# A mixture of experts whose three emptiest experts run with 64 slots

## The chip, the cores and the metric

The kernel runs on one core of one Trainium2 chip. The metric is the device time of one execution in microseconds (us), 1692.99 us as the median of three runs.

The engines are named as the profile names them: PE is TensorE's matrix multiply and PEld its weight load, DVE is VectorE, ACT is ScalarE, POOL is GpSimd and SP is SyncE. SP computes nothing here: its queue issues the loads of the weights.

## The reference

A trunk of two layers on 256 tokens of width 1024, all in float32. The first layer has a gated mixer with forgetting attention, memory cross-attention and a dense SwiGLU; the second has differential attention with a short convolution, memory cross-attention and a mixture of experts. The change lies in the last:

```python
def moe_swiglu(h, w_router, wg, wu, wd):            # h: 256 x 1024
    logits = t @ w_router                            # 8 experts
    top_v, top_i = lax.top_k(logits, 2)
    gates = softmax(top_v)
    combine = sum(one_hot(top_i, 8) * gates[..., None], axis=1)
    for e in range(8):                               # wg[e], wu[e]: 1024 x 3584, wd[e]: 3584 x 1024
        out += combine[:, e:e+1] * ((silu(t @ wg[e]) * (t @ wu[e])) @ wd[e])
```

Each token goes to two experts, so the eight experts share 512 places; on the inputs of the reference they get 42, 47, 42, 111, 102, 72, 34 and 62 tokens.

## The kernel before, in words

All matrix products take float32 data as pairs: a high part rounded to the fast matmul type (fp32r) and a low part, what is left. A product of two split operands is then three matmuls, high by high, high by low and low by high (`mm3`, lines 130 to 142). Activations are split once. Weights come from DRAM as float32 pieces of 1 MB into a buffer called raw, and `load_w` (lines 107 to 123) splits each piece: ACT writes the high part wh in two halves (line 118), DVE the low part wl in one instruction (line 120).

The experts run in the order 0 to 7, and each in seven chunks of 512 of its 3584 inner columns. For each expert the tokens are gathered into 128 slots by a matmul with a one-hot matrix (`slots`, `gather_pair`, `gained`, two experts at once), so that the tokens are the stationary operand, 128 slots wide, split into xgh and xgl, and the weights stream past as 512 columns. A chunk consists of:

- gate and up (`gate_up`): two weight pieces each, 8 matmul steps of 128x512 each, times three;
- `gated`: ACT takes silu of the gate sum and DVE multiplies the up sum into it, into sg, 128 slots x 512;
- `to_hT`: four PE transposes of sg into one PSUM bank (htp), from which ACT writes the high part of hs and DVE the low part (lines 126 and 127);
- `down`: two pieces of the down weights, 8 steps times three, into two PSUM banks that add up over the seven chunks.

In a chunk c the loop (line 1031 on) issues gate and up of c, then the loads and the down step of chunk c-1, then `to_hT` of c. The six pieces of a chunk are called g0, g1, u0, u1, d0 and d1 in the text. hs has a single buffer, so hs of a chunk is written when the down step before has read the last one. The order in which an engine issues its instructions is laid down when the program is built, from the data they need and the buffers that come free; it can differ from chunk to chunk, and each engine then keeps to it.

Buffers set the pace between the engines. Raw pieces go round a ring of 11 places (lines 996 and 997); SP issues a load when the piece that had the place has been split. Split pieces go round four pairs of wh and wl (line 999: three of the pool wsplit and one of wsplit2).

The first expert's slots are worked out in `route` from the router's logits: rank of each expert for each token, mask, and place of the token in its expert (pos). The gates (`gates`) follow in the second chunk. At the very end the largest count is taken (lines 1079 to 1084), every engine loads it as a number (line 1115), and a block that computes what does not fit into 128 slots is skipped when it is at most 128.

Of the kernel before, what the change touches and what calls it, by code (L numbers as in the profile page):

```python
# [20 lines left out]
P = 128  # L21
# [30 lines left out]
@with_exitstack  # L52
def trunk_kernel(ctx: ExitStack, tc: tile.TileContext, io, out, stop=None, cap=CAP):
    nc = tc.nc
# [150 lines left out]
    def route_consts():  # L205
        wr = cp.tile([P, KT, NE], F32, tag="wr", name="wr")
        nc.gpsimd.dma_start(wr, io["router_w"][0].rearrange("(k p) n -> p k n", p=P))
        gc = cp.tile([P, KT], F32, tag="gc", name="gc")
        gcr = t4([KT, P], "gcr")
        nc.gpsimd.dma_start(gcr, io["norm_ffn"][1].rearrange("(k p) -> k p", p=P))  # L210
        gcp = trp.tile([P, KT], F32, tag="tr", name="gcp")
        nc.tensor.transpose(gcp, gcr, ident[0:KT, 0:KT])
        nc.vector.tensor_copy(gc, gcp)
        nc.vector.tensor_tensor(wr, wr, gc[:, :, None].to_broadcast([P, KT, NE]), op=OP.mult)
        tri = cp.tile([P, NE, NE], F32, tag="tri", name="tri")
        nc.gpsimd.memset(tri, 1.0)
# [10 lines left out]
        return wr, gc, tri, ustr, ones, iota  # L227

    pA = ctx.enter_context(tc.tile_pool(name="acts", bufs=1))
    ps2 = ctx.enter_context(tc.tile_pool(name="xs", bufs=2))  # L230
    with ExitStack() as pre:
# [526 lines left out]
        with behind("resid", "Pool"):  # L758
            wr, gc, tri, ustr, ones, iota = route_consts()
        mem_v_half(1, 0)  # L760
# [3 lines left out]
    with ExitStack() as moe:  # L764
# [13 lines left out]
        lgs = mA.tile([P, 2, NE], F32, tag="lgs", name="lgs")  # L778
        rank = mA.tile([P, 2, NE], F32, tag="rank", name="rank")

        rht = pA.tile([P, 2, KT, P], F32, tag="V", name="rht")
# [6 lines left out]
        def route(t, acc):  # L788
# [53 lines left out]
            if t:  # L842
                with behind("pp"):
                    gather(0, 1)
                for i in range(2):
                    gather(1, i)

        def gates():
            for t in range(2):
# [16 lines left out]
                nc.vector.tensor_scalar(comb[:, t, 0:NE], s0, ge[:, 0:1], None, op0=OP.mult)  # L866
                nc.vector.scalar_tensor_tensor(comb[:, t, 0:NE], s1, ge[:, 1:2], comb[:, t, 0:NE], op0=OP.mult, op1=OP.add)

        def slots(dst, t, e):

            chain["DVE"] = nc.vector.tensor_scalar(dst, iota, pos[:, t, e:e + 1], None, op0=OP.is_equal)
            if cap < P:
                nc.vector.memset(dst.bitcast(F32)[..., cap:P], 0.0)

        def gained(kk, dst, src):

            dh, dl = (xg_all[i][:, dst, kk, :] for i in range(2))
            chain["ACT"] = nc.scalar.activation(dh, src, AF.Copy, scale=gc[:, kk:kk + 1])
            chain["DVE"] = nc.vector.scalar_tensor_tensor(dl, src, gc[:, kk:kk + 1], dh.bitcast(F32), op0=OP.mult, op1=OP.subtract)

# [3 lines left out]
        def gather_pair(e):  # L884
# [6 lines left out]
            for q in range(4):  # L891
# [4 lines left out]
                for k in range(2):  # L896
                    kk = 2 * q + k
                    sl = slice(kk * P, (kk + 1) * P)
                    for t in range(2):
                        nc.tensor.matmul(ps[:, k, :, :], xh[t][:, sl], se[:, t, :, :], start=t == 0, stop=False)  # L900
                        nc.tensor.matmul(ps[:, k, :, :], xl[:, t, sl], se[:, t, :, :], start=False, stop=t == 1)
                    gained(kk, slice(0, n), ps[:, k, 0:n, :])

# [27 lines left out]
        def gate_piece(w, e, c, half):  # L931
            return load_w(w[e, half * 512:(half + 1) * 512, c * 512:(c + 1) * 512]
                          .rearrange("(k p) n -> p k n", p=P), 4, 512)

        def gate_up(e, c, xg, ready=(), between=None):
# [3 lines left out]
            for w in (wg, wu):  # L939
# [4 lines left out]
                for half in range(2):  # L944
                    wh, wl = ready.pop(0) if ready else gate_piece(w, e, c, half)
                    mm = mm3([(ps, xgh[:, half * 4 + k, :], xgl[:, half * 4 + k, :], wh[:, k, :], wl[:, k, :])
                         for k in range(4)], False, half == 0, half == 1)
                res.append(ps)
                chain["PE"] = mm
            return res  # L950

        def gated(res, rs):
            sg = m2.tile([P, 512], F32, tag="sg", name="sg", bufs=1)
# [4 lines left out]
        def down_w(e, c, parts=1):  # L958
            return [load_w(wd[e, c * 512 + half * 256:c * 512 + half * 256 + 256, :]
                           .rearrange("(k p) n -> p k n", p=P), 2, D, parts) for half in range(2)]  # L960

        def to_hT(sg, pool=pA, tag="gain"):
            tp = mbank([P, 4, P], "htp")
# [7 lines left out]
        def down(c, hT, yacc, w2, ns=(0, 1)):  # L971
            hh, hl = hT
            return mm3([(yacc[n], hh[:, half * 2 + k, :], hl[:, half * 2 + k, :],
                  w2[half][0][:, k, n * 512:(n + 1) * 512], w2[half][1][:, k, n * 512:(n + 1) * 512])
# [42 lines left out]
        def final_gain():  # L1017
# [10 lines left out]
            return gf  # L1028

        prev = y = st = nrs = pyacc = gf = None  # L1030
        for e in range(NE):
            for c in range(nch):
# [28 lines left out]
                if prev is not None:  # L1061
                    w2 = down_w(*prev[:2])
                sg = gated(gu, rs)
                if prev is not None:
# [7 lines left out]
                if c == 0:  # L1072
                    yacc = [mmp.tile([P, 512], F32, tag="mm", name=f"y{n}") for n in range(2)]
                hT = to_hT(sg) if e + 1 < NE or c + 1 < nch else to_hT(sg, mA, "y")
                prev = (e, c, hT, yacc)
            xg, rs = xg_of(e % 2), nrs

        cc = mbank([P, NE], "cc")
        for t in range(2):
            nc.tensor.matmul(cc, ones, msk[:, t, :], start=t == 0, stop=t == 1)  # L1080
        cmax = sm.tile([P, 1], F32, tag="cmax", name="cmax")
        nc.vector.tensor_reduce(cmax, cc, axis=AX.X, op=OP.max)
        cint = mA.tile([1, 1], I32, tag="cint", name="cint")
        nc.vector.tensor_copy(cint, cmax[0:1, :])
        def finish(gf, before):
# [24 lines left out]
        def last_scatter(n):  # L1110
            scatter(pe, st, split_y(yacc, n, pA, ("gain", "K")[n]), n)
        finish(gf, last_scatter)


        cv = nc.values_load(cint[0:1, 0:1], min_val=0, max_val=S,
                            skip_runtime_bounds_check_because="a count of 256 tokens lies in 0..256")
        with tc.If(cv > cap):
            for e in range(NE):
                for r0 in range(cap, S, P):
                    se = mA.tile([P, 2, P], F32, tag="y", name="se_o")  # L1120
# [3 lines left out]
                    po = sm.tile([P, 2], F32, tag="po", name="po")  # L1124
                    nc.vector.tensor_scalar(po, pos[:, :, e], float(-r0), None, op0=OP.add)
                    for t in range(2):
# [24 lines left out]
                    for c in range(nch):  # L1151
                        sgs = []
                        for w in (wg, wu):
                            ps = accp.tile([P, 4, P], F32, tag="acc", name="gu_o")
                            raws = [load_raw(w[e, half * 512:(half + 1) * 512, c * 512:(c + 1) * 512]
                                             .rearrange("(k p) n -> p k n", p=P), 4, 512) for half in range(2)]
# [8 lines left out]
                        for half in range(2):  # L1165
                            rr = c * 512 + half * 256
                            rw = load_raw(wd[e, rr:rr + 256, :].rearrange("(k p) n -> p k n", p=P), 2, D)
                            for k in range(2):
# [43 lines left out]
```

## Time and profile before

| | us |
|---|---|
| runs, median of 3 | 1692.99 (1690.9 to 1695.35) |
| the profiled execution | 1696.55 |
| its span | 1694.7 |
| from the first gating of expert 0 to the last of expert 7 | about 661 to 1668 |

A profile is one execution of the program on the chip. Busy time of an engine is the time in which it ran instructions, idle time is put down to what released the next instruction. Matmuls overlap, so that PE can be counted busy while it does not run at its peak; the weight loads (PEld) show the pitch. The clock column is the share of TensorE's full clock that was granted. A load counts from its issue to its landing.

### The profile page before, as it was taken

How to read it: one execution, taken by the hardware profiler on the slowest of the kernel's cores; microseconds unless marked ns; L12 is line 12 of the kernel's file. 1: busy time of each engine (PE TensorE's matmuls, PEld its weight loads, DVE VectorE, ACT ScalarE, POOL GpSimd, SP SyncE). 2: the span in 40 equal slices, each digit the busy share in tenths (PEclk: the TensorE clock that was granted, in tenths of full speed). 3: DMA queues.
4: the chain of work that ended last, by engine and by line, in shares of the span. 5: the costliest groups of instructions: out<-in, count | busy, mean ns of one | idle time of the engine just before them, and what ended most of it. 6: DMA issues, size and time to landing. Idle time of an engine off the chain costs nothing. (4 is left out here: it accounts for less than half of the span.)

```text
span 1694.7 us, 22153 instructions
## 1 busy us (share of the span) xinstructions
PE 1649.0 (97%) x8700; PEld 1381.4 (82%) x8700; DVE 1273.6 (75%) x1170; ACT 1059.1 (62%) x1354; POOL 46.0 (3%) x64
## 2 busy tenths in 40 slices
PE   8999999999999999999999999999999999999996
PEld 7799889999988888888888777777778777778774
DVE  6686665444586657989888889788789878888876
ACT  6455554343564448877777676766667767677655
POOL 1000000000000102000000000000000000000000
PEclk9899999999999999999999999999999999999998
DMA  7446456565545577998998999999998999999970
GB/s 237 143 161 223 155 200 210 174 199 174 189 127 190 196 294 272 379 381 324 361 367 311 341 335 329 345 333 343 343 347 321 336 343 335 345 334 333 331 274 27
DMA packets 224556, 464.48 MB, mean 274 GB/s; under 512 B 9074, under 2 KB 64390, under 8 KB 224316
## 3 DMA queue, kind: packets, MB, share of 16 engines
q1 hardware_dynamic: 223564, 459.80, 76.2%
q0 software_dynamic: 880, 3.19, 0.5%
q8 instruction: 70, 1.15, 0.3%
q14 instruction: 42, 0.34, 0.1%
HBM read 461.90 MB, written 2.11 MB: 274 GB/s over the span
## 5 line engine op out<-in xcount | busy, mean ns | idle before, releaser
L120 DVE TENSOR_TENSOR wl<-raw,wh 128x2048 fp32r<-128x2048 f32 (+1 forms) x527 | 983.9, 1895 | 248.8 <-ACT wh L118 244.7
L118 ACT ACTIVATE wh<-raw 128x1024 fp32r<-128x1024 f32 x866 | 848.3, 1047 | 268.4 <-PE pws L138 92.0
L135 PE MATMUL gu<-wh,ch 128*128 128x512 f32 x896 | 357.0, 399 | 1.6 <-ACT wh L118 1.6
L138 PE MATMUL gu<-wh,cl 128*128 128x512 f32 x896 | 353.5, 395 | 0.0
L141 PE MATMUL gu<-wl,ch 128*128 128x512 f32 x896 | 250.3, 401 | 18.0 <-DVE wl L120 17.5
L141 PEld LDWEIGHTS gu<-wl,ch 128*128 128x128 f32 x896 | 162.2, 188 | 80.5 <-DVE wl L120 50.1
L135 PEld LDWEIGHTS gu<-wh,ch 128*128 128x128 f32 x896 | 169.0, 189 | 37.0 <-ACT wh L118 2.5
L138 PEld LDWEIGHTS gu<-wh,cl 128*128 128x128 f32 x896 | 169.0, 189 | 35.8
L135 PE MATMUL y<-wh,hs 128*128 128x512 f32 x448 | 179.3, 400 | 0.9 <-ACT wh L118 0.9
L138 PE MATMUL y<-wh,hs 128*128 128x512 f32 x448 | 177.0, 396 | 0.0
L135 PE MATMUL pws<-nh,wh 128*128 128x256 f32 x560 | 137.1, 283 | 0.0
L138 PE MATMUL pws<-nl,wh 128*128 128x256 f32 x560 | 137.1, 283 | 0.0
L126 ACT ACTIVATE hs<-htp 128x512 fp32r<-128x512 f32 x56 | 33.5, 598 | 142.1 <-PE y L141 116.9
L141 PE MATMUL y<-wl,hs 128*128 128x512 f32 x448 | 118.6, 395 | 0.0
L135 PEld LDWEIGHTS pws<-nh,wh 128*128 128x128 f32 x560 | 105.9, 189 | 1.3 <-ACT wh L118 0.9
L138 PEld LDWEIGHTS pws<-nl,wh 128*128 128x128 f32 x560 | 106.0, 189 | 0.4
L135 PEld LDWEIGHTS y<-wh,hs 128*128 128x128 f32 x448 | 84.3, 188 | 21.9 <-ACT wh L118 1.5
L141 PEld LDWEIGHTS y<-wl,hs 128*128 128x128 f32 x448 | 84.2, 188 | 19.4 <-issue 0.8
L138 PEld LDWEIGHTS y<-wh,hs 128*128 128x128 f32 x448 | 84.4, 188 | 18.5
L135 PE MATMUL acc<-wh,ch 128*128 128x512 f32 x216 | 84.8, 392 | 0.0
L138 PE MATMUL acc<-wh,cl 128*128 128x512 f32 x216 | 84.5, 391 | 0.0
L141 PE MATMUL pws<-nh,wl 128*128 128x256 f32 x560 | 78.9, 283 | 0.0
(329 smaller groups left out, 1786.5 us busy)
## 6 DMA issues: line engine op xcount, KB each, us to landing
raw<-in_moe_w_gate_dram SPq DMA_DIRECT2D x112, 1024.0 KB, 5.7
raw<-in_moe_w_up_dram SPq DMA_DIRECT2D x112, 1024.0 KB, 6.0
raw<-in_moe_w_down_dram SPq DMA_DIRECT2D x110, 1024.0 KB, 6.2
raw<-in_mem_w_kv_dram SPq DMA_DIRECT2D x16, 1024.0 KB, 5.4
raw<-in_odd_w_in_dram SPq DMA_DIRECT2D x12, 1024.0 KB, 5.2
raw<-in_ffn_w_gate_dram SPq DMA_DIRECT2D x11, 1024.0 KB, 5.2
raw<-in_ffn_w_up_dram SPq DMA_DIRECT2D x11, 1024.0 KB, 5.2
raw<-in_ffn_w_down_dram SPq DMA_DIRECT2D x11, 1024.0 KB, 4.8
```

What stands on the lines that cost most here:

```text
L118: chain["wh"] = nc.scalar.activation(hf[:, sl], rf[:, sl], AF.Copy)
L120: chain["wl"] = nc.vector.tensor_sub(lf[:, sl], rf[:, sl], hf[:, sl].bitcast(F32))
L126: return (nc.scalar.activation(hi, src, AF.Copy), nc.vector.tensor_sub(lo, src, hi.bitcast(F32)))
L135: mm = nc.tensor.matmul(ps, ah, bh, start=f, stop=False, skip_group_check=bank)
L138: nc.tensor.matmul(ps, *((ah, bl) if w_left else (al, bh)), start=False, stop=False, skip_group_check=bank)
L141: mm = nc.tensor.matmul(ps, *((al, bh) if w_left else (ah, bl)), start=False, stop=e, skip_group_check=bank)
```

## The change

The experts are put in order on the chip. `places` counts the tokens of each expert, ranks the experts by count (expert 0 always comes first) and spreads them over eight places: the three with the fewest tokens besides expert 0 come to places 2, 4 and 6. Positions, numbers, counts and gates are brought into that order, and SP loads the seven numbers into registers, from which it addresses the weights of places 1 to 7.

An expert at place 2, 4 or 6 has 64 slots. The one-hot matrix holds the 64 slots twice side by side; the high parts of the tokens go to columns 0 to 63 of the stationary tile and the low parts to columns 64 to 127. One matmul with wh and one with wl then give the sum for the high parts in rows 0 to 63 and for the low parts in rows 64 to 127, so two matmuls stand for three (`mm2`; the product of both low parts comes with them). `gated` copies both sums out, and `to_hT` multiplies them with a matrix of two stacked unit matrices (`twice`), which turns and adds the halves; gating and split follow on 64 columns a piece.

The fourth pair of split buffers goes, and the raw ring gets a twelfth place. The block for what does not fit starts at 64 slots for the small places.

```diff
-RAW2 = 3
+RAW2 = 4
+SCAP = 64
+SMALL = (2, 4, 6)
...
-        wp2 = moe.enter_context(tc.tile_pool(name="wsplit2", bufs=1))
...
-        pools["w"] = [wp] * 3 + [wp2]
...
+        def places():
+            cc = mbank([P, NE], "cc")
+            for t in range(2):
+                nc.tensor.matmul(cc, ones, msk[:, t, :], start=t == 0, stop=t == 1)
+            key = sm.tile([P, NE], F32, tag="s0", name="key")
+            nc.vector.scalar_tensor_tensor(key, cc, float(NE), iota[:, 0:NE], op0=OP.mult, op1=OP.add)
+            nc.vector.memset(key[:, 0:1], -1.0)
...
+            nc.vector.tensor_tensor(c1, key[:, None, :].to_broadcast([P, NE, NE]),
+                                    key[:, :, None].to_broadcast([P, NE, NE]), op=OP.is_lt)
...
+            nc.vector.tensor_reduce(rk, c1, axis=AX.X, op=OP.add)
+            nc.vector.tensor_tensor(pm, rk[:, None, :].to_broadcast([P, NE, NE]),
+                                    place[:, :, None].to_broadcast([P, NE, NE]), op=OP.is_equal)
+            for i, src in enumerate((pos[:, 0, :], pos[:, 1, :], iota[:, 0:NE], cc)):
+                c2 = sm.tile([P, NE, NE], F32, tag="c2", name="c2", bufs=1)
+                nc.vector.tensor_tensor(c2, pm, src[:, None, :].to_broadcast([P, NE, NE]), op=OP.mult)
+                nc.vector.tensor_reduce(byp[:, i, :], c2, axis=AX.X, op=OP.add)
...
+            nc.vector.tensor_copy(cint[:, 0:NE], byp[0:1, 2, :])
+            nc.vector.tensor_copy(cint[:, NE:NE + 1], over[0:1, 0:1])
+            for p in range(1, NE):
+                ids[p] = nc.values_load(cint[0:1, p:p + 1], engines=[mybir.EngineType.SP], min_val=0, max_val=NE - 1,
...
-            chain["DVE"] = nc.vector.scalar_tensor_tensor(dl, src, gc[:, kk:kk + 1], dh.bitcast(F32), op0=OP.mult, op1=OP.subtract)
+            for i in range(n):
+                if e + i in SMALL:
+                    dst = hi = dh[:, i, SCAP:P]
+                    rows = src[:, i, SCAP:P]
+                else:
+                    dst, hi, rows = dl[:, i, :], dh[:, i, :], src[:, i, :]
+                chain["DVE"] = nc.vector.scalar_tensor_tensor(dst, rows, g1, hi.bitcast(F32), op0=OP.mult, op1=OP.subtract)
...
-            return load_w(w[e, half * 512:(half + 1) * 512, c * 512:(c + 1) * 512]
+            return load_w(w[ids[e], half * 512:(half + 1) * 512, c * 512:(c + 1) * 512]
...
+        def mm2(jobs, first, last):
+            for which in range(2):
+                for i, (ps, a, *b) in enumerate(jobs):
+                    f = first and which == 0 and all(j[0] is not ps for j in jobs[:i])
+                    e = last and which == 1 and all(j[0] is not ps for j in jobs[i + 1:])
+                    mm = nc.tensor.matmul(ps, a, b[which], start=f, stop=e)
+            return mm
...
+            if e in SMALL:
+                sg = m2.tile([P, 2, 512], F32, tag="sgs", name="sgs", bufs=1)
+                for i in range(2):
+                    nc.scalar.activation(sg[:, i, :], res[i], AF.Copy, scale=rs)
+                return sg
...
+            if e in SMALL:
+                tp = mbank([P, 2, 4, SCAP], "htp")
+                for i in range(2):
+                    for k in range(4):
+                        nc.tensor.matmul(tp[:, i, k, :], sg[:, i, k * P:(k + 1) * P], twice, start=True, stop=True)
+                h = m2.tile([P, 4, SCAP], F32, tag="hsm", name="hsm", bufs=1)
+                nc.scalar.activation(h, tp[:, 0, :, :], AF.Silu)
+                nc.vector.tensor_tensor(h, h, tp[:, 1, :, :], op=OP.mult)
+                hs = pool.tile([P, 4, P], F32R, tag=tag, name="hs")
+                chain["hh"], chain["hl"] = split_to(hs[:, :, 0:SCAP], hs[:, :, SCAP:P], h)
+                return hs, None
...
                 if e == 0 and c in (1, 2):
                     with behind("wh", "wl"):
                         if c == 1:
+                            places()
                             gates()
```

## Rows read from the trace of the kernel before

**Rows 1.** The page: the span, and each engine's busy time and share of it.

```profile
span 1694.7 us, 22153 instructions
PE 1649.0 (97%) x8700; PEld 1381.4 (82%) x8700; DVE 1273.6 (75%) x1170; ACT 1059.1 (62%) x1354; POOL 46.0 (3%) x64
```

**Rows 2.** Stretches: length; busy PE, PEld, DVE, ACT, POOL; clock, DMA share, GB/s.

```profile
660.00:760.00 100.00, 100.00 (x460) 82.21 (x459) 92.01 (x83) 81.60 (x93) 0.00 (x0) 1.00 1.00 374
...
661.00:777.00 116.00, 116.00 (x538) 95.64 (x538) 105.89 (x95) 94.57 (x110) 0.00 (x0) 1.00 0.97 360
777.00:898.00 121.00, 121.00 (x543) 98.77 (x543) 105.93 (x67) 91.77 (x101) 0.00 (x0) 1.00 0.98 359
898.00:1027.00 129.00, 127.75 (x580) 102.71 (x579) 109.83 (x78) 91.11 (x108) 0.00 (x0) 1.00 0.91 328
1027.00:1158.00 131.00, 127.06 (x553) 99.13 (x552) 107.88 (x68) 89.94 (x102) 0.00 (x0) 1.00 0.94 338
```

**Rows 3.** Weight loads in order of time: start, duration, engine, line.

```profile
1107.94 0.19 PEld L135 LDWEIGHTS gu<-wh,ch 128*128 128x128 f32 x1
1108.17 0.19 PEld L138 LDWEIGHTS gu<-wh,cl 128*128 128x128 f32 x1
```

**Rows 4.** Groups by line from 640 us: count, busy us, mean ns, idle before.

```profile
L120 DVE TENSOR_TENSOR wl<-raw,wh 128x2048 fp32r<-128x2048 f32 x332 | 749.4, 2288 | 110.4 <-ACT wh L118 106.3 <-DMA raw<-in_moe_w_down_dram 1.5 <-PE y L141 1.2
...
L955 DVE SCALAR_TENSOR_TENSOR sg<-gu,rs,sg 128x512 f32<-128x512 f32 x56 | 41.8, 746 | 2.6 <-PE gu L141 2.5
L127 DVE TENSOR_TENSOR hs<-htp,hs 128x512 fp32r<-128x512 f32 x56 | 38.5, 687 | 14.4 <-ACT hs L126 14.4
...
L126 ACT ACTIVATE hs<-htp 128x512 fp32r<-128x512 f32 x56 | 33.5, 598 | 142.1 <-PE y L141 116.9 <-PE htp L965 24.9
L965 PEld LDWEIGHTS htp<-ident,sg 128*128 128x128 f32 x224 | 28.7, 140 | 9.0 <-DVE x L988 0.3
...
L879 DVE SCALAR_TENSOR_TENSOR cl<-xg,gc,ch 128x256 fp32r<-128x256 f32 x24 | 10.6, 480 | 3.9 <-ACT ch L878 3.9
```

**Rows 5.** Waits, 1027 to 1552 us: us in total, times, longest.

```profile
ACT hs L126 <- PE y L141: 88.7, 22, 4.7
...
PEld gu L141 <- DVE wl L120: 37.7, 58, 1.1
...
PE gu L141 <- DVE wl L120: 13.5, 35, 0.6
```

**Rows 6.** ACT in order of time: an early line, then a late chunk.

```profile
811.62 2.01 ACT L118 ACTIVATE wh<-raw 128x1024 fp32r<-128x1024 f32 x2 [0.74 <-PE gu L138]
...
1108.14 0.60 ACT L126 ACTIVATE hs<-htp 128x512 fp32r<-128x512 f32 x1 [3.70 <-PE y L141]
...
1114.25 0.69 ACT L954 ACTIVATE sg<-gu,rs 128x512 f32<-128x512 f32 x1 [1.73 <-PE gu L141]
1114.84 7.69 ACT L118 ACTIVATE wh<-raw 128x1024 fp32r<-128x1024 f32 x8
1126.47 0.60 ACT L126 ACTIVATE hs<-htp 128x512 fp32r<-128x512 f32 x1 [3.94 <-PE y L141]
```

**Rows 7.** SP's waits, 700 to 1600 us; a load: count, KB, us to landing.

```profile
SPq L103 <- DVE wl L120: 737.9, 281, 7.0
...
raw<-in_moe_w_up_dram SPq DMA_DIRECT2D x112, 1024.0 KB, 6.0
```

**Rows 8.** Groups: the router matmul, a small DVE operation, SP's load of a number.

```profile
L800 PEld LDWEIGHTS rlp<-wr,rht 128*128 128x128 f32 x32 | 4.0, 192 | 0.1
...
L867 DVE SCALAR_TENSOR_TENSOR comb<-s,ge,comb 128x8 f32<-128x8 f32 x2 | 0.4, 220 | 0.0
...
L1115 SPq TENSOR_LOAD <-cint x1: 1052/1052/1052, 1688.6 to 1688.6; - x1
```

**Rows 9.** Stretches near the end, columns as in rows 2.

```profile
1652.00:1654.00 2.00, 0.37 (x2) 0.30 (x2) 0.34 (x1) 1.94 (x3) 0.00 (x0) 0.99 0.00 0
1654.00:1656.00 2.00, 2.00 (x6) 1.60 (x5) 1.42 (x1) 2.00 (x3) 0.00 (x0) 0.50 0.00 0
```

More of the change, by code (lines that the diff above doesn't have):

```diff
@@ L52, in trunk_kernel @@
 @with_exitstack
[L53 removed]
+def trunk_kernel(ctx: ExitStack, tc: tile.TileContext, io, out, stop=None):
     nc = tc.nc
@@ L226, in route_consts @@
         nc.gpsimd.iota(iota, pattern=[[1, P]], base=0, channel_multiplier=0, allow_small_or_imprecise_dtypes=True)
-        return wr, gc, tri, ustr, ones, iota
+        iota2 = cp.tile([P, 2, SCAP], F32, tag="iota2", name="iota2")
+        nc.gpsimd.iota(iota2, pattern=[[0, 2], [1, SCAP]], base=0, channel_multiplier=0,
+                       allow_small_or_imprecise_dtypes=True)
+        place = cp.tile([P, 4, 2], F32, tag="place", name="place")
+        nc.gpsimd.iota(place, pattern=[[1, 4], [4, 2]], base=0, channel_multiplier=0,
+                       allow_small_or_imprecise_dtypes=True)
+        return wr, gc, tri, ustr, ones, iota, iota2.rearrange("p a b -> p (a b)"), place.rearrange("p a b -> p (a b)")
     pA = ctx.enter_context(tc.tile_pool(name="acts", bufs=1))
@@ L758, in trunk_kernel @@
         with behind("resid", "Pool"):
-            wr, gc, tri, ustr, ones, iota = route_consts()
+            wr, gc, tri, ustr, ones, iota, iota2, place = route_consts()
         mem_v_half(1, 0)
@@ L866, in gates, with gained @@
                 nc.vector.tensor_scalar(comb[:, t, 0:NE], s0, ge[:, 0:1], None, op0=OP.mult)
-                nc.vector.scalar_tensor_tensor(comb[:, t, 0:NE], s1, ge[:, 1:2], comb[:, t, 0:NE], op0=OP.mult, op1=OP.add)
+                nc.vector.scalar_tensor_tensor(s0, s1, ge[:, 1:2], comb[:, t, 0:NE], op0=OP.mult, op1=OP.add)
+                c2 = sm.tile([P, NE, NE], F32, tag="c2", name="c2", bufs=1)
+                nc.vector.tensor_tensor(c2, pm, s0[:, None, :].to_broadcast([P, NE, NE]), op=OP.mult)
+                nc.vector.tensor_reduce(comb[:, t, 0:NE], c2, axis=AX.X, op=OP.add)
         def slots(dst, t, e):
[L871 to L878, printed above, removed]
-            chain["DVE"] = nc.vector.scalar_tensor_tensor(dl, src, gc[:, kk:kk + 1], dh.bitcast(F32), op0=OP.mult, op1=OP.subtract)
+            at = byp[:, t, e:e + 1] if ids[1] is not None else pos[:, t, e:e + 1]
+            chain["DVE"] = nc.vector.tensor_scalar(dst, iota2 if e in SMALL else iota, at, None, op0=OP.is_equal)
+        def gained(kk, e, n, src):
+            dh, dl = (xg_all[i][:, 0:n, kk, :] for i in range(2))
+            g1 = gc[:, kk:kk + 1]
+            chain["ACT"] = nc.scalar.activation(dh, src, AF.Copy, scale=g1)
+            for i in range(n):
[5 more added lines that the diff above has]
+                chain["DVE"] = nc.vector.scalar_tensor_tensor(dst, rows, g1, hi.bitcast(F32), op0=OP.mult, op1=OP.subtract)
         def xg_of(i):
@@ L972, in down @@
             hh, hl = hT
+            if hl is None:
+                return mm2([(yacc[n], hh[:, half * 2 + k, :], w2[half][0][:, k, n * 512:(n + 1) * 512],
+                             w2[half][1][:, k, n * 512:(n + 1) * 512])
+                            for half in range(2) for n in ns for k in range(2)], c == 0, c == nch - 1)
             return mm3([(yacc[n], hh[:, half * 2 + k, :], hl[:, half * 2 + k, :],
@@ L1028, in final_gain @@
             return gf
+        twice = mA.tile([P, SCAP], F32, tag="twice", name="twice")
+        for i in range(2):
+            nc.gpsimd.tensor_copy(twice[i * SCAP:(i + 1) * SCAP, :], ident[i * SCAP:(i + 1) * SCAP, i * SCAP:(i + 1) * SCAP])
         prev = y = st = nrs = pyacc = gf = None
@@ L1073, in trunk_kernel @@
                     yacc = [mmp.tile([P, 512], F32, tag="mm", name=f"y{n}") for n in range(2)]
-                hT = to_hT(sg) if e + 1 < NE or c + 1 < nch else to_hT(sg, mA, "y")
+                hT = to_hT(e, sg) if e + 1 < NE or c + 1 < nch else to_hT(e, sg, mA, "y")
                 prev = (e, c, hT, yacc)
             xg, rs = xg_of(e % 2), nrs
[L1078 to L1084, printed above, removed]
         def finish(gf, before):
```

43 lines of the change are left out of this document (29 added, 14 removed).

## The prediction

> **What bounds the kernel now.** The page comes first [rows 1]: span 1694.7 us, TensorE (PE) busy for 97% of it. The change touches only the last part, the experts, so I cut that by expert [rows 2], where an expert is seven chunks. Its first two stretches last 116 and 121 us with PE busy throughout; the fourth lasts 131, with PE busy 127, VectorE (DVE) 108, ScalarE (ACT) 90 and 338 GB/s of loads. One order of instructions thus runs at 121/7 = 17.3 us a chunk, and another at 131/7 = 18.7.
>
> The pitch of the matmuls tells which of the two is PE's own pace: weight loads follow each other every 0.23 us [rows 3]. A chunk has 72 of these matmuls, 72 x 0.23 = 16.6, and four transposes at 28.7/224 = 0.13 [rows 4] make 17.1. So the early chunks are bound by PE, and the late ones lose about 1.4 us each. The waits name the loss [rows 5]: in four experts ACT stands 88.7 us waiting for the end of the down matmuls before it evicts hs, and PE stands 37.7 + 13.5 us behind DVE's low parts, which follow ACT's high parts. In order of time [rows 6], ACT comes to hs after eight half-splits and waits 3.7 to 3.9 us there; the splits behind it start late.
>
> Loads bind nothing yet. SP's queue waits 737.9 us of 900 for raw buffers that DVE has to free [rows 7], so the ring of 11 (lines 996 and 997) is always full. One turn of it lasts 11 x 131/42 = 34 us; about 6 go to the landing [rows 7], 2.1 to ACT's two halves and 2.3 to DVE, so some 24 us of landed weights lie ahead (about 20 at the early pace).
>
> **Small experts, PE.** In the 21 chunks of experts 2, 4 and 6 the 24 matmuls with the low token part go: 24 x 0.23 = 5.5 us. The four transposes (0.6) become eight fp32 matmuls of 64 columns. The nearest row is the router's fp32 matmul [rows 8]: two records for each of the sixteen in the code, 4.0 us of weight loads for 32, so 0.25 a matmul and 2.0 for eight. PE's chunk becomes 11.0 + 2.0 = 13.0 us, 4.2 less: 88 us over the kernel, which PE alone would give. It is not collected whole, because others come next.
>
> **Small experts, the others.** The six pieces of a chunk are still loaded and split. DVE loses the 512-wide gating (0.75) and the low part of hs (0.69) and gets two of half the width, for which the 480 ns of a 256-wide form stand [rows 4]: 0.5 less a chunk, so 107.9 - 3.4 = 104.5 us of work an expert. ACT loses 0.69 [rows 6] + 0.60 and gets two 512-wide copies (0.60 each [rows 4]) and two of 256 (0.48 each, as DVE's): 0.9 more, 96 us an expert. The loads are 42 pieces of 1.049 MB, 44.0 MB; at the 374 GB/s that 100 us show [rows 2] that is 118 us, of which the 20 us ahead in the ring may be borrowed; the large expert behind it pays them back. A small and a large one together have to take 2 x 118 = 236; 115.5 + 131 = 246 do.
>
> So DVE is next. Back to back it gives 104.5. With today's idle time on top, 131 - 107.9 = 23.1 [rows 2], it gives 127.6. That idle time follows ACT's waits for PE, 3.7 to 3.9 at hs and 1.7 at sg [rows 6], 5.5 a chunk, and PE is done 4.2 earlier; but ACT still comes to hs in the middle of its splits. I take half of it, 104.5 + 11 = 115.5, the middle, since one cause shrinks and the order that makes the other stays. Against (129 + 131 + 131)/3 = 130.3 now that is 14.8 less, **-44 us** for three, with ends of -77 and -8.
>
> One rule on loads speaks against this. The rows hold 374 GB/s over 100 us. The Trainium skill, "DMA: Bandwidth & Descriptors", section "Where 436 GB/s comes from", says that for loads from HBM the limit is about 358 GB/s a core. By it a small expert without borrowing would take 123 us and the term would be -22; the trace does not agree with the limit, having passed it for 100 us.
>
> **Routing.** `places` puts 18 small DVE instructions and `gates` four more into the second chunk: at the 0.22 us of their like [rows 8] 4.8 us. The three pair gathers get eight more DVE instructions each, for the halved side, each at most half of the 0.48 [rows 4]: 6 us, partly beside PE. DVE is busy 106 of 116 us in that first expert [rows 2], so I count 4 of the 11; ends 0 and 11. SP loads seven numbers at 1.05 us each [rows 8], 7.4 us in its queue, and first waits for `places`; queued behind are the loads of the later chunks, and behind those ACT. The 20 us of landed weights cover that: 0, and 8 if the ring is still filling there. Addresses from a register cost SP no more than part of its 2.8 us a piece: 0. The count at the end (two matmuls, two DVE instructions) went beside the last splits: 0. **+4 us.**
>
> **Buffers.** The fourth pair of split buffers goes; the raw ring gets a twelfth place (more cushion, 0). In the late order a pair is free in time even with three: behind sg at 1114.25 ACT splits u1, d0, d1 and the next g0, eight halves at 0.96 us from 1114.84 on [rows 6]; d0 starts at 1116.8 and needs the pair of g1, three pieces before, and sg itself waited for PE to end g1. So three pairs would cost it nothing. In the early order ACT already waits 0.74 us for PE before a piece [rows 6]; it could fall to the late pace, at most 5 x 1.4 + 7 x 1.4 = 17 us over the first two experts. From the other side, a new order can have the early pace in experts 3, 5 and 7, 20 chunks x 1.4 = 28 less. I take **+3**, near no change because the rows of the late order show none; ends -28 and +17.
>
> **Sum.** -44 + 4 + 3 = -37 against the profiled execution's own 1696.55 us, that is 1659.5; the median of the runs is 3.6 us lower, so 1656.
>
> **The rivals.**
> Faster still: the splits are ordered anew and the ACT waits at hs go. Large experts then take 121 (-28) and small ones 236 - 121 = 115, held by loads: -44 + 4 - 28 = -68, 1625; with 107 for the small ones, if loads run above 374, -70 + 4 - 28 = -94, 1599. For it: the first experts do run so [rows 2]. Against: one pair less of room.
>
> Gain mostly lost: the chain ACT, DVE, PE keeps its idle time, or the loads do not follow, and a small expert takes about 124: -19 + 4 + 3 = -12, 1681. For it: DVE, loads and ACT all have 96 to 118 us of work in an expert, so any wait shows. The limit on loads that the Trainium skill states would put it about here. Against: PE's 29 us are gone from every small one.
>
> Slower: the missing pair. Its place is the down step, which holds two pairs for 5.5 us, so that one piece alone can be ready behind it, in all 35 large chunks. The price is between nothing and one DVE split (2.29 us [rows 4]) a chunk. It decides from (44 - 4)/35 = 1.1 us on; at the whole split it is 80 - 40 = +40, 1733; at 1.4 us, +9, 1702. For it: PE already waits for the low part with four pairs [rows 5]. Against: the order in rows 6 never needs four.
>
> Slower by the clock: PE will idle some 3 us in a small chunk. Clock 0.50, that is 1.2 of 2.4 GHz, was granted at 1654 us, after a stretch in which PE was busy 0.37 of 2 us [rows 9]; the late experts, with pauses of up to 1.1 us, kept 1.00 [rows 2, 5]. If it fell in the small chunks, PE would need 26 us a chunk, 3 x 7 x (26 - 18.6) = +155, 1850; it decides where more than 0.6 of that time is at the low level. The Trainium skill, "TensorE: Matmul & The Clock Gate", section "A second HAM failure mode: psum-queue depth-cycling", describes matmul groups with frequent short pauses between which the clock swings; no run here shows that for pauses of a microsecond.
>
> It may also not do what it says: an expert among the three with over 64 tokens would start the overflow block, hundreds of us. The reference's router, worked out on its inputs, gives 42, 47, 42, 111, 102, 72, 34 and 62 tokens; the three fewest besides expert 0 have 34, 42 and 47, so it does not start.
>
> **How the numbers follow.** Forecast, 1632 to 1672: 0.47. Faster still, 1599 to 1632: 0.20. Gain mostly lost, 1672 to 1688: 0.15. No change: 0.05, where 0.3% (5 us) is about what a measurement of this kernel can tell. Missing pair: 0.09; clock: 0.03; overflow: 0.01. Faster is 0.47 + 0.20 + 0.15 = 0.82, slower 0.13. The range leaves out the slower cases, the unchanged one and the very end of the fast one: 1612 to 1690.
>
> **What would show it.** Right: stretches of about 115 us for experts 2, 4 and 6 and 131 for 3 and 5; in the small ones 8 matmuls a piece instead of 12; no wait on a load; granted clock 1.00. Wrong: small experts at 125 or more with DVE idle behind ACT, or under 107; large ones off by over 10 us from 131; PE or ACT waiting for raw loads around 680 us, which would put the seven register loads on the path.

## The result, and the profile after

The changed kernel takes **1675.62 us** (median of 4, 1674.53 to 1679.09) against 1694.17 for the kernel before on the same chip: ratio 0.9894 (95% interval 0.987 to 0.9919), 18.6 us or 1.1% faster. The forecast was 1656, twice that gain. The profiled execution took 1674.53 us.

The page of the changed kernel, first the span, then the engines' busy time:

```profile
span 1672.8 us, 22375 instructions
PE 1581.7 (95%) x8448; PEld 1300.4 (78%) x8448; DVE 1263.6 (76%) x1214; ACT 1077.1 (64%) x1396; POOL 46.9 (3%) x68
```

Against [rows 1] PE lost 67 us of work and the span 22. To see where it stuck I cut the experts at the point where DVE first splits hs in each. These are the stretches of experts 0 to 6 (columns as in [rows 2]):

```profile
657.00:776.00 119.00, 119.00 (x555) 98.38 (x554) 111.05 (x128) 96.21 (x111) 0.00 (x0) 1.00 0.97 353
776.00:898.00 122.00, 120.99 (x548) 98.35 (x546) 107.71 (x70) 93.51 (x103) 0.00 (x0) 1.00 1.01 364
898.00:1022.00 124.00, 109.14 (x493) 79.28 (x494) 105.69 (x86) 95.00 (x118) 0.00 (x0) 1.00 0.97 342
1022.00:1153.00 131.00, 124.52 (x543) 96.10 (x543) 108.33 (x70) 91.33 (x105) 0.00 (x0) 1.00 0.98 341
1153.00:1280.00 127.00, 111.22 (x502) 80.47 (x501) 108.04 (x86) 97.69 (x122) 0.00 (x0) 1.00 0.97 343
1280.00:1410.00 130.00, 123.52 (x539) 95.34 (x538) 107.33 (x69) 90.33 (x103) 0.00 (x0) 1.00 0.96 342
1410.00:1538.00 128.00, 111.78 (x502) 80.56 (x502) 106.55 (x78) 97.19 (x122) 0.00 (x0) 1.00 0.95 344
```

The small experts (third, fifth, seventh line) take 124 to 128 us where 115.5 was forecast. No engine is full in them: PE is idle for 15 to 16 us, DVE for 18 to 21, ACT for 29 to 31. The clock is 1.00 throughout. The same cuts in all traces, which the experiments come back to (us; expert 7 is counted up to its last chunk):

```
expert                    0     1     2     3     4     5     6     7
kernel before         118.7 121.5 128.4 130.1 131.6 130.1 131.6 115.7
changed kernel        118.8 122.2 123.9 130.7 126.9 130.7 127.9 112.2
e2_no_low             118.3 117.5 124.5 129.5 124.6 129.5 125.6 115.6
e5_four_pairs         119.5 123.9 127.4 130.6 127.4 130.7 128.2 114.5
e6_no_small           119.0 121.4 129.2 128.9 132.4 128.9 131.5 113.1
e1_half_loads         118.9 120.8 104.4 120.5 104.4 120.5 102.3 105.7
e3_copies_late        118.8 122.1 111.6 132.5 111.7 132.6 112.1 112.2
e4_all_late           118.9 127.0 111.4 137.7 111.5 137.6 111.7 112.2
e7_large_silu_late    118.8 122.0 111.7 129.0 111.8 129.1 110.9 109.0
e8_large_hs_late      123.4 117.8 114.6 123.0 114.6 123.0 113.7 102.6
e9_before_late        122.6 119.8 126.6 123.5 126.3 123.5 126.1 107.2
e11_best              123.2 117.9 114.7 123.0 114.6 123.0 113.7 102.6
e12_best_later        127.4 113.6 120.0 118.3 120.1 118.3 119.2  98.0
```

The cut goes by hs. Where an edit moves hs of some experts (e4, e8, e9, e11, e12), the cut moves with it and shifts some us between neighbours; there only the sum of a large expert and the small one behind it can be compared.

The three small experts gained 4.5 + 4.7 + 3.7 = 12.9 us; experts 0, 1, 3 and 5 lost 2.0, expert 7 gained 3.5. That makes 14.4; each large expert counted with the small one behind it, the three pairs gained 11.0 of it. The end behind the last chunk gave back 1 us. The rest of the profiled gain is not the change's: the first gate matmul of the experts starts at 646.61 us before and at 638.08 after, 8.5 earlier, and the clock did that. Stretches of the kernel before, then of the changed one:

```profile
46.00:53.00 7.00, 7.00 (x18) 4.75 (x18) 3.44 (x5) 3.29 (x3) 0.00 (x0) 0.52 0.63 221
640.00:647.00 7.00, 6.68 (x32) 6.39 (x32) 4.47 (x13) 4.01 (x6) 5.01 (x4) 0.51 0.61 202
```

```profile
46.00:53.00 7.00, 7.00 (x30) 4.42 (x28) 5.07 (x7) 3.29 (x3) 0.00 (x0) 1.00 0.59 207
640.00:647.00 7.00, 7.00 (x33) 5.76 (x32) 5.78 (x4) 4.83 (x5) 3.14 (x3) 1.00 0.76 258
```

A clock of 0.52 and 0.51, that is the level of 1.2 GHz, came in those stretches before and not after. `e10_after_again` shows that it differs between executions of the same kernel.

The loss inside a small chunk stands in ACT's and DVE's instructions in order of time (start, duration, and in brackets the idle time ahead of it and what ended it):

```profile
934.88 0.69 ACT L1019 ACTIVATE sgs<-gu,rs 128x512 f32<-128x512 f32 x1 [1.72 <-PE gu L991]
935.46 3.89 ACT L120 ACTIVATE wh<-raw 128x1024 fp32r<-128x1024 f32 x4
941.08 0.69 ACT L1019 ACTIVATE sgs<-gu,rs 128x512 f32<-128x512 f32 x1 [1.73 <-PE gu L991]
941.66 1.99 ACT L120 ACTIVATE wh<-raw 128x1024 fp32r<-128x1024 f32 x2
943.56 0.37 ACT L1038 ACTIVATE hsm<-htp 128x256 f32<-128x256 f32 x1
943.82 2.00 ACT L120 ACTIVATE wh<-raw 128x1024 fp32r<-128x1024 f32 x2
947.27 0.42 ACT L128 ACTIVATE hs<-hsm 128x256 fp32r<-128x256 f32 x1 [1.44 <-PE y L991]
947.59 3.89 ACT L120 ACTIVATE wh<-raw 128x1024 fp32r<-128x1024 f32 x4
953.19 0.69 ACT L1019 ACTIVATE sgs<-gu,rs 128x512 f32<-128x512 f32 x1 [1.71 <-PE gu L991]
...
937.49 4.50 DVE L122 TENSOR_TENSOR wl<-raw,wh 128x2048 fp32r<-128x2048 f32 x2 [1.70 <-ACT wh L120]
943.69 2.29 DVE L122 TENSOR_TENSOR wl<-raw,wh 128x2048 fp32r<-128x2048 f32 x1 [1.71 <-ACT wh L120]
...
939.84 1.20 PE L991 MATMUL gu<-wl,ch 128*128 128x512 f32 x4 [0.89 <-DVE wl L122]
```

Three times a chunk ACT stands in front of an eviction, 1.72, 1.73 and 1.44 us. What it waits for is the last product of a piece, which needs DVE's low part of that piece, which needs the high part that ACT itself split just before. Follow one turn: the copy at 934.88 holds ACT for 0.58; the two halves of the next piece take 2.0; DVE starts the low part at 937.49 and takes 2.29; PE's last products, from 939.84, take 1.3 with the start; the next copy starts at 941.08. That is 6.20 us. The next turn ends with hs at 947.27, 6.19 us later, and the third with the copy at 953.19, 5.92 later: together 18.31 us, the whole chunk. Of PE's work only 1.3 us of each turn lie on this path, the four products with the low part of the weights, and these the change leaves as they were. So 4.2 us less of PE's work changes nothing in such a chunk. Not every chunk is like this: cut at hs, the second of expert 4 takes 15.0 us (17.9 before) and the last 15.2 (16.6 before), and there most of the small experts' gain lies.

The waits of expert 2 say the same (us in total, times, longest):

```profile
DVE wl L122 <- ACT wh L120: 19.0, 15, 1.7
PEld gu L991 <- DVE wl L122: 16.9, 17, 1.2
ACT sgs L1019 <- PE gu L991: 16.3, 10, 1.7
```

### The profile page after: what moved, and what is told of

Read it like the earlier page. It is cut to its first block, busy times and chain, and to the rows that moved or that the text cites. A ratio compares the mean times of both kernels' runs of the same rounds, so it can differ in the third digit from the quotient of the medians.

```text
span 1672.8 us, 22375 instructions
## 1 busy us (share of the span) xinstructions
PE 1581.7 (95%) x8448; PEld 1300.4 (78%) x8448; DVE 1263.6 (76%) x1214; ACT 1077.1 (64%) x1396; POOL 46.9 (3%) x68
## 5 line engine op out<-in xcount | busy, mean ns | idle before, releaser
L137 PE MATMUL gu<-wh,ch 128*128 128x512 f32 x560 | 222.0, 397 | 0.0
L140 PE MATMUL gu<-wh,cl 128*128 128x512 f32 x560 | 219.4, 392 | 0.1
L143 PE MATMUL gu<-wl,ch 128*128 128x512 f32 x560 | 155.8, 400 | 11.9 <-DVE wl L122 11.7
L991 PE MATMUL gu<-wl,ch 128*128 128x512 f32 x336 | 98.8, 416 | 40.1 <-DVE wl L122 40.1
L140 PEld LDWEIGHTS gu<-wh,cl 128*128 128x128 f32 x560 | 105.2, 188 | 22.2 <-DVE cl L1097 0.5
L137 PE MATMUL y<-wh,hs 128*128 128x512 f32 x280 | 112.9, 403 | 0.3 <-ACT wh L120 0.3
L140 PE MATMUL y<-wh,hs 128*128 128x512 f32 x280 | 110.4, 394 | 0.0
L991 PE MATMUL gu<-wh,ch 128*128 128x512 f32 x336 | 99.9, 403 | 1.5 <-ACT wh L120 1.3
L143 PE MATMUL y<-wl,hs 128*128 128x512 f32 x280 | 74.6, 396 | 0.0
```

What stands on the lines that cost most here:

```text
L137: mm = nc.tensor.matmul(ps, ah, bh, start=f, stop=False, skip_group_check=bank)
L140: nc.tensor.matmul(ps, *((ah, bl) if w_left else (al, bh)), start=False, stop=False, skip_group_check=bank)
L143: mm = nc.tensor.matmul(ps, *((al, bh) if w_left else (ah, bl)), start=False, stop=e, skip_group_check=bank)
L991: mm = nc.tensor.matmul(ps, a, b[which], start=f, stop=e)
```

## The experiments

Theory A is this order of ACT's instructions. Theory B is the loads: 342 to 344 GB/s at a DMA share of 0.97. Rival C is that the new form of the gating, with two copies more on ACT, eats its own gain.

**e1_half_loads**, each load of a small expert half as large:

```
-        r = load_raw(src, a, b, parts)
+        r = load_raw(src[:, 0:a // 2, :], a // 2, b) if hf_only else load_raw(src, a, b, parts)
...
+                        chain["wh"] = nc.scalar.activation(hf[:, sl], rf[:, 0:m], AF.Copy)
...
```

> Edit to the changed kernel: in the three small experts each load brings half of its 1 MB, and both halves of a split read that half (half of these experts' weights is left out). Theory A (ACT's order: it stands 1.44, 1.72 and 1.73 us of a chunk of 18.4 in front of evictions whose matmuls wait for DVE's low part): the chunks of the small experts stay at 18.3 to 18.6 us, the experts at 124 to 128 us, the time within 4 us of 1675.6. Theory B (the transfers bind: 344 GB/s at a DMA share of 0.97): 6.3 MB a chunk become 3.1, the chunk falls to DVE's 14.6 busy us, some 26 us less for each small expert, 1597 us.

1586.07 us, one run; 104 us for a small expert. Taken alone that speaks for B. But the large experts, whose loads are whole, fell to 120.5 as well, and the order of the instructions is another one. It is laid down when the kernel is built, and it came out otherwise with this edit. ACT in a small chunk:

```profile
918.85 2.01 ACT L122 ACTIVATE wh<-raw 128x1024 fp32r<-128x1024 f32 x2 [0.36 <-DVE wl L124]
920.77 0.67 ACT L1026 ACTIVATE sgs<-gu,rs 128x512 f32<-128x512 f32 x1
921.34 2.00 ACT L122 ACTIVATE wh<-raw 128x1024 fp32r<-128x1024 f32 x2
923.51 2.01 ACT L122 ACTIVATE wh<-raw 128x1024 fp32r<-128x1024 f32 x2 [0.18 <-PE gu L998]
925.42 0.67 ACT L1026 ACTIVATE sgs<-gu,rs 128x512 f32<-128x512 f32 x1
```

Both copies find their sums done and start without a wait. So the run doesn't separate A from B. It shows what a chunk takes with DVE back to back, for whatever reason: 13.88 us.

**e2_no_low**, the kernel before without the matmuls of the low token part:

```
-                nc.tensor.matmul(ps, *((ah, bl) if w_left else (al, bh)), ...)
+                if low:
+                    nc.tensor.matmul(ps, *((ah, bl) if w_left else (al, bh)), ...)
```

> The kernel before with one edit: for experts 2, 4 and 6 the matmuls of the low part of the tokens are left out (these outputs lack that product); nothing is ordered, all buffers and evictions are those of before. It is the change's saving on TensorE alone. Theory A (the loop ACT, DVE, PE sets the chunk in whatever form the evictions have): experts 2, 4 and 6 fall from 128.4, 131.6 and 131.6 us by 3 to 8 each, 1672 to 1685 us. Rival C (the changed kernel loses the gain to its own two extra copies and its longer way to hs): here the gain comes out, 115 to 118 us for each, 1645 to 1655. Besides it shows whether the clock falls to 0.50 ahead of the experts as it did in the profiled execution of before (46 to 63 and 640 to 647 us, some 8 us late at the experts' first matmul against the changed kernel).

1670.7 us, one run. Experts 2, 4 and 6 take 124.5, 124.6 and 125.6, as in the changed kernel: A has it right and C falls, for here nothing of the new form is there. (Expert 1's last chunk, which by these cuts reaches into expert 2, gained 4 us.) The total is 1.3 under A's range. The waits over experts 3 to 6, two of which are without 5.5 us of PE's work in each chunk, in the kernel before (the window of [rows 5]) and then in this one (1016 to 1526 us):

```profile
DVE wl L120 <- ACT wh L118: 61.9, 53, 2.2
...
ACT hs L126 <- PE y L142: 79.5, 22, 4.6
DVE wl L120 <- ACT wh L118: 61.4, 54, 2.2
```

DVE stands behind ACT as long as before, and ACT's 88.7 us at hs [rows 5] lost 9.2.

**e3_copies_late**, only the place of the two copies:

```
-                for i in range(2):
-                    nc.scalar.activation(sg[:, i, :], res[i], AF.Copy, scale=rs)
+                with behind("wh"):
+                    for i in range(2):
+                        nc.scalar.activation(sg[:, i, :], res[i], AF.Copy, scale=rs)
```

> Edit to the changed kernel: ACT's two copies of the gate and up sums of a small expert stand behind the chunk's last split, in place of between the splits. Theory A: two of the three waits of 1.7 us go, a chunk falls from 18.4 to 16.5 to 17.2 us, 21 of them give 25 to 40 us, 1636 to 1651 us. Theory B (transfers, or anything but this order): no change, 1672 to 1680. Between (the wait comes back at hs, which now stands one piece behind the copies): 17.5 to 18, 1660 to 1668.

**1639.44 us**, ratio 0.9696 (0.9679 to 0.9712) to the kernel before; small experts 112. This separates the theories: whole loads, the same work, and a chunk of 18.3 falls to 14.9, below the 16.5 to 17.2 that A expected (16.0 on average over the expert); the total lies in A's range. ACT, then expert 2 as a stretch and its waits:

```profile
935.54 7.68 ACT L120 ACTIVATE wh<-raw 128x1024 fp32r<-128x1024 f32 x8
943.13 1.25 ACT L1020 ACTIVATE sgs<-gu,rs 128x512 f32<-128x512 f32 x2
944.28 2.00 ACT L120 ACTIVATE wh<-raw 128x1024 fp32r<-128x1024 f32 x2
947.97 0.39 ACT L1039 ACTIVATE hsm<-htp 128x256 f32<-128x256 f32 x1 [1.70 <-PE htp L1037]
```

```profile
906.00:1017.00 111.00, 102.93 (x492) 80.05 (x491) 104.36 (x83) 93.28 (x118) 0.00 (x0) 1.00 1.01 378
```

```profile
ACT hsm L1039 <- PE htp L1037: 7.4, 6, 1.7
...
DVE wl L122 <- ACT wh L120: 4.9, 6, 1.0
```

DVE's wait for ACT is 4.9 us in place of 19.0, and the loads ran at 378 GB/s. The 342 of the changed kernel was what the splits asked for, not what the loads could give.

**e4_all_late**, the same, and the transposes, Silu and hs of a small expert in the next chunk:

```
+                        with behind("wh"):
+                            prev = (*prev[:2], prev[2](), prev[3])
...
-                hT = to_hT(e, sg) if e + 1 < NE or c + 1 < nch else to_hT(e, sg, mA, "y")
+                hT = partial(to_hT, e, sg)
...
```

> The edit of e3_copies_late, and the transposing matmuls, the Silu and the split of hs of a small expert moved into the next chunk, behind the split of its second gate piece. Theory A: the third wait, 1.44 us for the last y matmuls, goes too: a chunk takes 15.0 to 16.8 us (DVE is busy 14.6; 6.3 MB at the 374 GB/s of the fastest stretch before take 16.8), 35 to 60 us less than the changed kernel, 1616 to 1641. Theory B: no change, 1672 to 1680. If the loads take over as soon as the order lets them: 16.8 to 17.5, 1640 to 1655, with ACT waiting for raw and the 12 us between landing and use gone.

1653.45 us, 0.9782 (0.9766 to 0.9798): 14 us worse than e3_copies_late. Neither theory had it; the time lies in the third range, where the loads take over, but the sign named for that did not come: ACT waited 1.2 us in all for landings. Later is not better without end: the transposes now stand behind the next chunk's gate matmuls, and ACT waits for them instead,

```profile
954.11 0.38 ACT L1040 ACTIVATE hsm<-htp 128x256 f32<-128x256 f32 x1 [2.81 <-PE htp L1038]
```

so a chunk of 14.9 takes 16.0 to 16.3, and a large expert with the small one behind it takes 5 us more (249.2 against 244.2 for experts 3 and 4). That the table puts it all at the large one is the cut, which moved with hs.

**e5_four_pairs**, a fourth pair of split buffers for two raw places:

```
-RAW2 = 4
+RAW2 = 2
+        wp2 = moe.enter_context(tc.tile_pool(name="wsplit2", bufs=1))
+        pools["w"] = [wp] * 3 + [wp2]
```

> Edit to the changed kernel: four pairs of wh and wl again, ten places for raw weights in place of twelve. Prediction's step 5 and its rival of the missing pair: the large experts, 130.7 us in the changed kernel against 130.1 before, lose their wait and fall by 2 to 6 each, 1650 to 1666. Theory A (the order of ACT's evictions sets the chunk; a pair more does not move it): large experts 129 to 132, small 123 to 128, 1672 to 1681.

1688.98 us, 0.9978 (0.9961 to 0.9995). The large experts stay at 130.6, and the small ones, at 127.4 to 128.2, do not fall: the fourth pair, with two raw places fewer, gains nothing. The total is outside A's range and worse than the changed kernel's, by experts 1, 2 and 7; whether the two raw places or another order did that was not separated.

**e6_no_small**, the routing and the buffers alone:

```
-SMALL = (2, 4, 6)
+SMALL = ()
...
```

> Edit to the changed kernel: no expert is small; the experts are ordered by their counts, the loads go by registers, three pairs and twelve raw places stay. It is the routing and the buffers alone. Against the changed kernel the three small experts go back to the 128 to 132 us of before: plus 13 us, 1685 to 1691, and 1684 to 1694 against 1691 for the kernel before, that is no difference. If the routing or the seven register loads cost anything that shows, expert 0 and 1 take more than 119 and 122 us, and it comes out above 1696.

1691.82 us, 0.9982 (0.9961 to 1.0002), no difference. Experts 0 and 1 take 119.0 and 121.4: ordering and register loads cost nothing that can be seen, nor do three pairs in place of four: experts 3 and 5 take 128.9, against 130.1 before.

**e7_large_silu_late**, e3_copies_late with the Silu of a large expert moved too:

```
-            nc.scalar.activation(sg, res[0], AF.Silu, scale=rs)
+            with behind(*(("d0",) if "d0" in chain else ())):
+                nc.scalar.activation(sg, res[0], AF.Silu, scale=rs)
...
+                chain[f"d{half}"] = chain["wh"]
...
```

> The edit of e3_copies_late, and for the large experts ACT's Silu of the gate sum stands behind the split of the first down piece (it stood behind that of the first up piece, where it waited for the low product of the second gate piece). Theory A: experts 3, 5 and 7 fall from 132.5 towards the 122 of expert 1, whose chunks (17.2 us) have that order already; 8 to 28 us less than e3_copies_late, 1611 to 1632. Theory B (the loads: 44.0 MB at the 378 GB/s of the small experts of e3_copies_late take 116.5 us per expert, the small ones ran at 111.6 on what the ring had ahead): no more than 10 us, 1630 to 1640, and the small experts go up as the large ones come down.

1629.92 us, 0.9631 (0.9593 to 0.9668). The large experts fell by 3.5 only, though the wait at sg is gone; the one at hs stayed:

```profile
1074.04 0.68 ACT L1024 ACTIVATE sg<-gu,rs 128x512 f32<-128x512 f32 x1
...
1081.87 0.60 ACT L128 ACTIVATE hs<-htp 128x512 fp32r<-128x512 f32 x1 [3.37 <-PE y L143]
```

It lies at the seam of the two ranges, so it does not decide; the small experts did not go up, which speaks against B.

**e8_large_hs_late**, and hs of a large expert behind the second gate piece of the next chunk:

```
+                    if hT is not None and w is wg and half == 1:
+                        with behind("wh"):
+                            hT()
...
```

> The edit of e7_large_silu_late, and a large expert's transposes and the split of hs moved behind the split of the second gate piece of the next chunk. Theory A: ACT's waits of up to 3.94 us for the transposes go as well, another 0 to 10 us against e7_large_silu_late, 1605 to 1630. Against it: hs comes later, and the y products of the next chunk may wait for it: then equal or up to 10 us slower.

**1617.83 us**, 0.9546 (0.9517 to 0.9576). The time is in A's range. Large experts take 123.0 and small ones 3 us more than in e7, but the cut moved with hs: a large expert and the small one behind it took 240.8 in e7 (experts 3 and 4) and take 237.6 here.

**e9_before_late**, the kernel before with the two edits for large experts:

```
-            nc.scalar.activation(sg, res[0], AF.Silu, scale=rs)
+            with behind(*(("d0",) if "d0" in chain else ())):
+                nc.scalar.activation(sg, res[0], AF.Silu, scale=rs)
...
-                hT = to_hT(sg) if e + 1 < NE or c + 1 < nch else to_hT(sg, mA, "y")
+                hT = partial(to_hT, sg)
...
```

> The kernel before with the order of e8_large_hs_late from expert 1 on: Silu of the gate sum behind the split of the first down piece, transposes and hs behind the split of the next chunk's second gate piece; no small experts. Theory A (the order kept all late experts, large ones too, off TensorE's pace): the chunks of experts 2 to 6 fall from 17.8 to 19.1 us to 17.1 to 17.5, an expert from 130 to 121 to 124, 30 to 50 us in all, 1644 to 1664 us. Theory B (in the kernel before something else, the loads or TensorE itself, held them): 1685 to 1695. What then remains between this kernel and the best one with small experts is the change's own worth when the order lets it: 30 to 45 us.

1661.56 us, 0.9791 (0.9755 to 0.9827), in A's range. The order held the kernel before as well. Experts 3 and 5 fall to 123.5, as expected; experts 2, 4 and 6 only to 126.1 to 126.6, and the reason was not looked for. Expert 3:

```profile
1034.00:1158.00 124.00, 123.90 (x552) 99.74 (x550) 107.80 (x69) 91.11 (x104) 0.00 (x0) 1.00 0.98 361
```

PE is busy all the time, against 127.06 of 131 in [rows 2].

**e10_after_again**, no edit:

> The changed kernel as it is, on this chip: 1673 to 1685 us; its experts 2, 4 and 6 at 124 to 128 us in the trace whatever the clock does ahead of the experts. If the 8 us that its first profile was early at the experts' first matmul are the clock's and not the change's, they are not there in every run: with clock grants of 0.50 at 45 to 63 and 636 to 645 us as in the kernel before, the time is 1680 to 1685.

1681.09 us, 0.9903 (0.9869 to 0.9937). The experts take what they took (123.9, 127.0 and 128.0 for the small ones), but the clock falls ahead of them this time, and their first matmul is at 646.70, where the kernel before had it. Its span, 1682.0 us, is 12.7 under that of before, where the clock fell at about the same places: that is the change with the clock alike. The medians, 17 to 19 us apart, are of executions whose mean granted clock differs from 0.987 to 0.996.

```profile
45.00:61.00 16.00, 16.00 (x37) 10.11 (x36) 7.03 (x10) 4.21 (x7) 0.00 (x0) 0.50 0.52 169
642.00:645.00 3.00, 2.81 (x13) 2.81 (x14) 2.48 (x6) 2.56 (x3) 1.85 (x2) 0.51 0.94 319
```

**e11_best**, e8 with expert 0 left in its old order:

```
-                if not (e not in SMALL and (e + 1 < NE or c + 1 < nch)):
+                if not (e and e not in SMALL and (e + 1 < NE or c + 1 < nch)):
```

> The kernel of e8_large_hs_late with expert 0 left in its old order (that run's expert 0 took 123.4 us in place of 118.8): 3 to 7 us less than e8_large_hs_late's 1617.8 if the loads still have room, 1609 to 1616; if the loads bind throughout (377 GB/s at a DMA share of 1.00 to 1.02 there), what expert 0 gives up is paid later, 1615 to 1620.

1619.15 us, 0.9538 (0.9508 to 0.9568): the same as e8, and both beat the two kernels by 3 to 5%. The edit had nothing to gain: expert 0 still takes 123.2, its last chunk 21.6 in place of 17.2, because the first late hs, that of expert 1, moves the cut; experts 0 and 1 together take 241.1, against 241.0 in the changed kernel. So the time, though in the range for binding loads, does not show that they bind. Experts 2 and 3:

```profile
904.00:1019.00 115.00, 106.40 (x506) 82.77 (x506) 107.57 (x86) 97.16 (x122) 0.00 (x0) 1.00 1.01 377
1019.00:1142.00 123.00, 120.29 (x537) 95.61 (x535) 107.33 (x70) 91.78 (x104) 0.00 (x0) 1.00 1.00 365
```

**e12_best_later**, hs of a large expert yet a piece later:

```
-                    if hT is not None and w is wg and half == 1:
+                    if hT is not None and (w is wg and half == 1 if c in (4, nch - 1) else w is wu and half == 0):
```

> The kernel of e11_best with hs of a large expert behind the split of the first up piece, where the order of experts 0 and 1 has it, in place of the second gate piece: between 8 us faster and 4 slower than e11_best, 1603 to 1618; no change if the loads bind.

1622.26 us, 0.9561 (0.9526 to 0.9596), no better, and 4 above the range. Experts 3 and 5 come down to 118.3 and the last chunks of experts 2 and 4 take 23.6 in place of 18.2, which is the cut again: experts 3 and 4 take 238.4 together, against 237.6. What bounds this order was not tried. The engines waited for landings for 1.2 us in all in e11_best and for 3.7 here, at a DMA share of 0.99 to 1.02.

## Why the prediction was wrong, and where it was right

**The step that failed** is in the first term of the sum, the -44 for the small experts. It lies in the idle time, the 11 us in this sentence: "I take half of it, 104.5 + 11 = 115.5, the middle, since one cause shrinks and the order that makes the other stays." The work was right: DVE is busy 105.7 to 108.0 us in a small expert, ACT 95.0 to 97.7 (104.5 and 96 forecast). The idle time was not: 18 to 21 of the 23.1 us stayed, not 11, and the three small experts gained 12.9 us in place of 44. I took ACT's waits as waits for PE, so that PE's being done 4.2 us earlier had to shorten them. But the row "ACT hs <- PE y" [rows 5] names only the last link. In the changed kernel a low part of DVE's stands in front of it, and in front of that ACT's own split of the same piece. In the kernel before that is so at sg; at the hs of 1126.47 us [rows 6] the last pause of PE for a low part is at 1119.22, and from there on PE worked through, so that PE's own work stood over the loop:

```profile
1119.22 1.18 PE L141 MATMUL gu<-wl,ch 128*128 128x512 f32 x4 [0.43 <-DVE wl L120]
```

With 5.5 us of that work gone from a chunk, ACT's waits at hs fell only from 88.7 to 79.5 us (e2_no_low). The rows for the loop were there: PE behind DVE's low parts [rows 5], and ACT's standing at sg right after the halves of a piece [rows 6]. e2_no_low shows that taking PE's work away, and nothing else, leaves 124.5 to 125.6; e3_copies_late that moving two copies, with no work less, gives 112. The sign named for wrong, 125 or more with DVE idle behind ACT, came in two of the three small experts.

What came true is the rival **gain mostly lost**, at its "about 124" and by the first of its two reasons; the second, the loads, was not it. I gave it 0.15. The range, 1612 to 1690, holds the time.

**PE.** The eight transposing matmuls were put at 2.0 us a chunk. Their weight loads take 41.1 us in 21 chunks, 1.96:

```profile
L1036 PEld LDWEIGHTS htp<-twice,sgs 128*128 128x128 f32 x336 | 41.1, 191 | 15.2 <-ACT sgs L1019 13.0 <-DVE ch L929 1.4
```

**Routing**, +4: nothing that shows in e6_no_small, which has the ordering and the register loads but no halved side in the gathers; the gathers were not tried apart. The cover named for SP's seven loads, landed weights, held: expert 0 takes 118.8 us, against 118.7 before.

**Buffers**, +3: experts 0, 1, 3 and 5 lost 2.0 us together. The argument from the late order, that it never needs a fourth pair, held. The rival of the missing pair falls with e6_no_small, which has three pairs and no small expert and is no slower than the kernel before.

**Loads.** They were no bound: SP's queue still waits for DVE to free places, as in [rows 7],

```profile
SPq L105 <- DVE wl L122: 626.0, 258, 7.2
```

no engine waited for landings for more than 1.6 us in all, and in e3_copies_late a small expert at 111.6 us drew 378 GB/s. The Trainium skill, "DMA: Bandwidth & Descriptors", section "Where 436 GB/s comes from", has about 358 GB/s a core as the limit from HBM; the trace of e3_copies_late passes it for 111 us. That sentence in the prediction (a term of -22) came nearer to the time than mine by accident.

**Clock.** It stayed at 1.00 in the small experts with pauses of PE of up to 1.2 us, so that rival falls.

**Faster still** did not come by itself: the build gave the small chunks three waits in place of two, and the large ones their old order. Given by hand, it does: 1618 lies in that rival's 1599 to 1632. Its pair of 121 and 115 came as 123.0 and 114.6; that loads hold the small ones, as it has it, is not shown.

**What the change is worth** depends on the order around it. On one chip: before 1697.91, the change alone 1681.09 (17 us less), the order alone 1661.56 (36 less), both 1619.15 (79 less). With the order mended first, the change brings 1661.56 - 1619.15 = 42 us. That this is near the 37 forecast is luck: the forecast left the order as it was.

## What to carry to other kernels

A wait's row names the last link only. Before a saving on the engine that is waited for is counted, follow one turn of the loop back to the engine that waits: if the turn comes back to it, the saving counts only by what it takes from the turn (here PE has 1.3 of 6.2 us in it, and the change took nothing from those). In this kernel ACT works in a fixed order and has both to evict sums and to prepare operands. There it paid to let it come to an eviction a piece or two later than the sum's own last operand (e3_copies_late), and not later still (e4_all_late, e12_best_later). Without the change that was worth 36 us, about twice the change alone.

## What was not expected of the hardware

The clock's grants ahead of the experts differ from run to run of the same kernel: from 17 to 552 us the first trace of the changed kernel shows 1.00, the second 0.50 from 45 to 61 and 0.51 from 642 to 645, and the experts' first matmul is 8.6 us later in it (646.70 against 638.08). What PE did ahead does not tell them apart: it was busy for 8.84 of the 10 us from 35 to 45 where the clock then fell to 0.50, the level of 1.2 GHz, and for 9.19 of the same 10 where it stayed. And a core drew 377 to 379 GB/s from memory over whole small experts (e3_copies_late, e11_best), at a DMA share of 1.01 to 1.02.
